# GpSimd adds the mean row of the normalised tiles, and the residual's moves are dealt out 6, 6, 6, 6, 5, 3

## The chip, the cores and the metric

The kernel runs on one core of a Trainium2 chip. The metric is the device time of one execution in microseconds (us); the figure for a kernel is the median of its runs. The engines are TensorE (PE in the profile, with its weight loads as PEld), VectorE (DVE), ScalarE (ACT), GpSimd (POOL) and SyncE (SP), which here only issues transfers. Each engine works through its own instructions in the order in which they were put there; an instruction whose inputs are not ready holds up everything behind it on that engine.

## The reference, cut to what matters

One decoder layer on 256 tokens of width 2048, with 16 meta tokens ahead of them: sparse attention and causal pooling side by side, an output map, a layer norm, a gated feed-forward block with a causal convolution of width 3, and a second layer norm.

```python
mix = jnp.concatenate([attn_out, pool_out], axis=-1) @ w_o[l]
h = layer_norm(ALPHA * h + mix, ln1_g[l], ln1_b[l])
f = conv_gated_ffn(h, w_up[l], conv_w[l], conv_b[l], w_down[l])
h = layer_norm(ALPHA * h + f, ln2_g[l], ln2_b[l])

def layer_norm(x, g, b):
    mu = jnp.mean(xf, axis=-1, keepdims=True)
    var = jnp.mean(jnp.square(xf - mu), axis=-1, keepdims=True)
    return (xf - mu) * lax.rsqrt(var + LN_EPS) * g + b
```

The change lies between the first layer norm and the end of the up-projection's first third.

## The kernel before, in words

Features lie on the 128 partitions and tokens along the free axis: `y` (the profile calls it x) holds 16 tiles `y[:, m]` of 128 features x 272 tokens. Every fp32 weight block `wraw` of 128x2048 comes in by a 1 MB transfer from SP, is rounded by ACT in two halves of 1024 columns (L162) into the high part of `whl`, and DVE subtracts the high part from the raw weight for the low part (L163), also in two halves. There are three `whl` buffers. A product (L202 to L204) then runs 16 steps k of three matmuls each: high x high, high x low, low x high. So the third matmul of a product waits for the first L163 of its block.

The up-projection has 44 steps f with two halves each (`half_` 0 and 1), one weight block and 48 matmuls for each half. The norm of the first layer norm is not ready when the first up-projections start. The first four f (`FOLDED = 4`) therefore multiply weights with the tiles `folded`, which hold the values before the norm times the gain, and `unfold` puts the norm in behind the product: `u = ps * rs` on DVE (L731), a row `w` from ACT (L733), and `u = u + w` on GpSimd (L734). `rs` is the row of reciprocal deviations, `m2` the row of minus mean times that; both are halves of the tile `of_token`, written by ACT at L695. The convolution starts with L721 on ACT, which reads `u`, and goes on with L722 and L723 on DVE; `gate` follows (L738, L739).

Meanwhile `normalise(m)` makes the real inputs `hp` of the later up-projections, three tiles after each half of the first f: a multiplication by `rs` on GpSimd (L703), an addition of `m2` on DVE (L704), gain and offset on ACT (L705), the high part on ACT (L707), the low part on DVE (L708). They are first used by f = 4.

At f = 4 and 5 the 16 tiles of `y` are transposed in blocks of 32x32 on DVE (L869). At f = 6 to 11, `residual` carries the transposed blocks into `y2`, the accumulator of the output with tokens on partitions, in 32 transfers issued on ACT's queue (L715): the list `moves` has the 16 for the first 128 tokens ahead of the 16 for the others. The down-projection of the first eight f runs between the up-projections of the next eight (`seven`); its results are added into `y2` by DVE at L799, which therefore waits for these transfers.

The order on each engine comes from a scheduler that works with its own priorities and estimates, so instructions written in one place may stand elsewhere in the queue. What belongs to a product, and so its weight block, is told below by f and half: f1h1 is the second half of f = 1.

Of the kernel before, what the change touches and what calls it, by code (L numbers as in the profile page):

```python
# [14 lines left out]
ALU = mybir.AluOpType  # L15
# [21 lines left out]
FOLDED = 4  # L37
# [61 lines left out]
def tile_layer(ctx, tc, xt, w_first, w_proj, w_uk, w_uv, w_pool, w_o, w_up, w_down, cols, rows, rel_bias, onehot, out):  # L99
    nc = tc.nc  # L100
# [4 lines left out]
    def act_tile(name, n=T):  # L105
        t = ring.tile([P, SLOT], F32R, tag="act", name=name)
        u, l = NARROW if n < T else (0, T)
        return Pair(t[:, u:u + n], t[:, l:l + n])
# [4 lines left out]
    def big():  # L113
        return pm.tile([P, 512], F32, tag="mm", name="mm")
# [75 lines left out]
    def weights(ahead=2):  # L190
        i = state["use"]
        state["use"] += 1
        prefetch(i + 1 + ahead)
        return ready.pop(i)

    def product(ps, hl, m, act, lo, hi, ks=range(KT), width=P, k0=0, k1=KT):

        for n in range(k0, k1):
            k = ks[n]
            wh, wl = hl[:, 0, k * width:k * width + m], hl[:, 1, k * width:k * width + m]  # L200
            ah, al = act[k][:, 0, lo:hi], act[k][:, 1, lo:hi]
            nc.tensor.matmul(ps, wh, ah, start=n == 0, stop=False)  # L202
            nc.tensor.matmul(ps, wh, al, start=False, stop=False)  # L203
            nc.tensor.matmul(ps, wl, ah, start=False, stop=n == KT - 1)  # L204
# [36 lines left out]
    def col(base, j):  # L241
        return cv[:, base + j:base + j + 1]
# [31 lines left out]
    for i in range(2):  # L274
        nc.vector.tensor_tensor(kidx[DI * i:DI * i + DI, 1 + i, :], ps[:DI, :T], kidx[:DI, 0, :].bitcast(F32),
                                op=ALU.subtract)
# [356 lines left out]
    rs, m2 = of_token[:, :NQ], of_token[:, NQ:]  # L633
# [42 lines left out]
    def deviation():  # L676
        ps = small()
        column_sums([s1], cuts, 0, ps)
        column_sums([s2], cuts, 1, ps)
        for i, (a, b) in enumerate(cuts):  # L680
            r = slice(0, b - a)
            nc.vector.tensor_scalar_mul(st[r, 0, i:i + 1], ps[r, 64 * i:64 * i + 1], 1.0 / D)
            nc.vector.tensor_scalar(st[r, 1, i:i + 1], ps[r, 64 * (3 + i):64 * (3 + i) + 1], 1.0 / D, EPS,
                                    op0=ALU.mult, op1=ALU.add)
        nc.vector.tensor_tensor(st[:, 2, :], st[:, 0, :], st[:, 0, :], op=ALU.mult)
        nc.vector.tensor_tensor(st[:, 1, :2], st[:, 1, :2], st[:, 2, :2], op=ALU.subtract)
        nc.vector.tensor_tensor(st[:2, 1, 2:], st[:2, 1, 2:], st[:2, 2, 2:], op=ALU.subtract)
        nc.gpsimd.tensor_tensor(st[:, 2, :], st[:, 1, :], half, op=ALU.pow)
        nc.vector.scalar_tensor_tensor(st[:, 3, :], st[:, 0, :], -1.0, st[:, 2, :], op0=ALU.mult, op1=ALU.mult)

    def deviation_rows():
        for j, dst in ((2, rs), (3, m2)):
            ps = small()
            spread(st[:, j, :], cuts, ps)
            nc.scalar.activation(dst, ps[:, :NQ], AF.Copy)  # L695
# [5 lines left out]
    def normalise(m):  # L701
        yd = y[:, m, Q0:]
        nc.gpsimd.tensor_tensor(yd, yd, rs, op=ALU.mult)  # L703
        nc.vector.tensor_tensor(yd, yd, m2, op=ALU.add)  # L704
        nc.scalar.activation(yd, yd, AF.Identity, bias=col(LN1, 2 * m + 1), scale=col(LN1, 2 * m))  # L705
        a = act_tile("hp", NQ)
        nc.scalar.activation(a[:, 0, :NQ], yd, AF.Copy)  # L707
        nc.vector.tensor_tensor(a[:, 1, :NQ], yd, a[:, 0, :NQ].bitcast(F32), op=ALU.subtract)  # L708
        h_parts.append(a)
# [9 lines left out]
    def conv(j, half_, src, za):  # L719
        z = fp.tile([P, S], F32, name="z", tag="z1", bufs=1) if half_ else za  # L720
        nc.scalar.activation(z, src[:, 2:NQ], AF.Identity, bias=col(C_B, j), scale=col(C_W, 3 * j + 2))  # L721
        nc.vector.scalar_tensor_tensor(z, src[:, 1:NQ - 1], col(C_W, 3 * j + 1), z, op0=ALU.mult, op1=ALU.add)  # L722
        nc.vector.scalar_tensor_tensor(z, src[:, :S], col(C_W, 3 * j), z, op0=ALU.mult, op1=ALU.add)  # L723
        return z

    def unfold(ps):

        sc = fp.tile([P, 2], F32, name="sc", tag="sc")
        nc.vector.tensor_copy(sc, ps[:, NQ:NE])
        u = fp.tile([P, NQ], F32, name="u", tag="sq")  # L730
        nc.vector.tensor_tensor(u, ps[:, :NQ], rs, op=ALU.mult)  # L731
        w = fp.tile([P, NQ], F32, name="w", tag="acc", bufs=2)
        nc.scalar.activation(w, m2, AF.Identity, bias=sc[:, 1:], scale=sc[:, :1])  # L733
        nc.gpsimd.tensor_tensor(u, u, w, op=ALU.add)  # L734
        return u

    def gate(za, zg):
        nc.scalar.activation(za, za, AF.Gelu_apprx_tanh)  # L738
        nc.vector.tensor_tensor(za, za, zg, op=ALU.mult)  # L739

    def two_parts(a, src):
        nc.scalar.activation(a[:, 0], src, AF.Copy)
        nc.vector.tensor_tensor(a[:, 1], src, a[:, 0].bitcast(F32), op=ALU.subtract)
        return a
# [7 lines left out]
    def forms(p, r, j):  # L752

        a11, a21, a12, a22 = r[:, 0, :P], r[:, 0, P:], r[:, 1, :P], r[:, 1, P:]
        s = fp.tile([P, 4 * P], F32, name="forms", bufs=1).rearrange("p (a b) -> p a b", b=P)
        nc.gpsimd.tensor_tensor(s[:, 0], a21, a22, op=ALU.add)
        nc.gpsimd.tensor_tensor(s[:, 2], s[:, 0], a11, op=ALU.subtract)
        nc.gpsimd.tensor_tensor(s[:, 1], a12, s[:, 2], op=ALU.subtract)
        nc.gpsimd.tensor_tensor(s[:, 3], a11, a21, op=ALU.subtract)  # L759
        left = two_parts(slot(), r[:, :, :P])  # L760
        mid = two_parts(slot(), s[:, :2])
        right = ring.tile([P, SLOT], F32R, tag="act", name="right")
        right = Pair(*(right[:, o:o + 2 * P].rearrange("p (b c) -> p b c", c=P) for o in (0, T)))
        right = two_parts(right, s[:, 2:])
        if p == PLAIN[0]:
            lone, i = two_parts(slot(), r[:, :, P:]), 1
        else:
            if j % 2 == 0:
                held["lone"] = slot()
            lone, i = held["lone"], j % 2  # L770
            two_parts(lone[:, :, i], a22)
        return {"P1": (left, 0), "P2": (left, 1), "P5": (mid, 0), "P3": (mid, 1), "P6": (right, 0),
                "P7": (right, 1), "P4": (lone, i), "a21": (lone, 0)}
# [52 lines left out]
    for item in plan:  # L826
        if item[0] in "ABC":
            seven(*item)
            continue
        _, f, half_ = item  # L830
        part = next(p for p in range(len(PARTS)) if f < sum(PARTS[:p + 1]))
        if half_ == 0:
            if f % 2 == 0:
                pair = fp.tile([P, 2, S], F32, name="za", tag="z0", bufs=3)
            both = []
        hl = weights()
        ps = big()
        if todo and f > FOLDED - 1 + half_:
            p, r = todo.pop(0)
            pairs[p].append(forms(p, r, len(pairs[p])))  # L840
        if f < FOLDED:
            k = 0
            if f + half_ == 0:
                product(ps[:, :NE], hl, P, folded, 0, NE, k1=7)
                deviation()
                product(ps[:, :NE], hl, P, folded, 0, NE, k0=7, k1=14)
                deviation_rows()
                k = 14
            product(ps[:, :NE], hl, P, folded, 0, NE, k0=k)
            while len(h_parts) < min(KT, 3 * (2 * f + half_ + 1)):  # L850
                normalise(len(h_parts))
            both.append(ps)
            if half_ == 0:
                continue
            both = [conv(i * FT + f, i, unfold(both[i]), pair[:, f % 2]) for i in range(2)]
        else:
            product(ps[:, :NQ], hl, P, h_parts, 0, NQ)
            both.append(conv(half_ * FT + f, half_, ps, pair[:, f % 2]))
            if half_ == 0:
                continue  # L860
        gate(*both)
        if part == len(PARTS) - 1:
            a = fp.tile([P, 2, NE], F32R, name="gp", tag="gp", bufs=19)
            gated.append(two_parts(a[:, :, :S], both[0]))
        elif f % 2:
            todo.append((part, pair))
        if f in (FOLDED, FOLDED + 1):
            for m in range(8 * (f - FOLDED), 8 * (f - FOLDED) + 8):
                nc.vector.transpose(y[:, m, NM:], y[:, m, NM:])  # L869
        if FOLDED + 2 <= f < FOLDED + 8:  # L870
            for _ in range((6, 5, 5)[f % 3]):
                residual(*moves.pop(0))


# [176 lines left out]
```

## Time and profile before

| what | us |
|---|---|
| runs, median (lowest to highest of 3) | 1038.26 (1037.95 to 1040.22) |
| the profiled execution's own time | 1039.8 |
| its span, first to last instruction | 1038.0 |
| PE busy in the span | 1025.3 (99%) |
| DVE / ACT / POOL busy | 886.1 (85%) / 617.4 (59%) / 209.3 (20%) |

The profiled execution is 1.5 us above the median and 1.8 us above its own span. Its granted TensorE clock is 0.998 of full over the span. Times in the profile count from the span's first instruction. In rows of the timeline the first column is the start, the second the length (of all the instructions that the row merges, up to the end of the last), x is their count, and the bracket gives the idle time of the engine ahead of it and what ended it. Ends of matmuls are modelled, so stalls of PE are better read from the distance of starts than from its busy share.

### The profile page before, as it was taken

How to read it: one execution, taken by the hardware profiler on the slowest of the kernel's cores; microseconds unless marked ns; L12 is line 12 of the kernel's file. 1: busy time of each engine (PE TensorE's matmuls, PEld its weight loads, DVE VectorE, ACT ScalarE, POOL GpSimd, SP SyncE). 2: the span in 40 equal slices, each digit the busy share in tenths (PEclk: the TensorE clock that was granted, in tenths of full speed). 3: DMA queues.
4: the chain of work that ended last, by engine and by line, in shares of the span. 5: the costliest groups of instructions: out<-in, count | busy, mean ns of one | idle time of the engine just before them, and what ended most of it. 6: DMA issues, size and time to landing. Idle time of an engine off the chain costs nothing.

```text
span 1038.0 us, 19165 instructions
## 1 busy us (share of the span) xinstructions
PE 1025.3 (99%) x7649; PEld 973.8 (94%) x7649; DVE 886.1 (85%) x1372; ACT 617.4 (59%) x994; POOL 209.3 (20%) x262
## 2 busy tenths in 40 slices
PE   9999999999999999999999999999999999999996
PEld 8998999999999999998999999999999999999985
DVE  6879468758779997898999999899998998999866
ACT  7566356645447765565566655656555656566654
POOL 1100014125345311211122011120111201110022
PEclk9999999999999999999999999999999999999999
DMA  9766543454552587898798787887878878898766
GB/s 326 259 216 236 194 156 109 152 188 167 191 196 85 200 233 248 261 301 257 260 299 293 283 283 271 287 284 274 286 269 288 276 277 278 269 306 274 277 203 152
DMA packets 59610, 250.80 MB, mean 242 GB/s; under 512 B 21718, under 2 KB 22400, under 8 KB 32384
## 3 DMA queue, kind: packets, MB, share of 16 engines
q1 hardware_dynamic: 34016, 229.37, 61.5%
q0 software_dynamic: 8320, 17.71, 8.9%
q10 hardware_dynamic: 17184, 2.49, 1.4%
q8 instruction: 60, 0.98, 0.4%
q14 instruction: 30, 0.25, 0.1%
HBM read 233.55 MB, written 3.16 MB: 228 GB/s over the span
## 4 chain that ended last, share of the span: by engine, by line
PE 82%; DVE 7%; issue 5%; DMA 4%; POOL 1%; ACT 1%; DVEq 0%; POOLq 0%; ACTq 0%
PE mm L204 20%; PE mm L203 20%; PE mm L202 20%; PE at L792 5%; PE at L793 5%; PE at L791 5%; DVE whl L163 3%; DMA wraw<-in_w_down 2%; DMA wraw<-in_w_up 1%; DMA y<-x 1%; DVE x L704 1%; ACT whl L162 1%; DVE hp L708 1%; PE mm L265 1%; PE mm L267 1%
## 5 line engine op out<-in xcount | busy, mean ns | idle before, releaser
L163 DVE TENSOR_TENSOR whl<-wraw,whl 128x1024 fp32r<-128x1024 f32 (+1 forms) x418 | 492.7, 1213 | 53.8 <-ACT whl L162 52.9
L162 ACT ACTIVATE whl<-wraw 128x1024 fp32r<-128x1024 f32 (+1 forms) x418 | 405.0, 1014 | 147.4 <-DVE wraw L158 39.6
L204 PE MATMUL mm<-hp,whl 128*128 128x258 f32 x1280 | 360.8, 282 | 0.0
L203 PE MATMUL mm<-hp,whl 128*128 128x258 f32 x1280 | 359.7, 281 | 0.0
L202 PE MATMUL mm<-hp,whl 128*128 128x258 f32 x1280 | 355.5, 278 | 0.0
L202 PEld LDWEIGHTS mm<-hp,whl 128*128 128x128 f32 x1280 | 240.7, 188 | 3.1
L203 PEld LDWEIGHTS mm<-hp,whl 128*128 128x128 f32 x1280 | 239.6, 187 | 3.0
L204 PEld LDWEIGHTS mm<-hp,whl 128*128 128x128 f32 x1280 | 240.2, 188 | 0.0
L202 PE MATMUL mm<-xp,whl 128*128 128x256 f32 (+5 forms) x384 | 110.9, 289 | 0.0
L203 PE MATMUL mm<-xp,whl 128*128 128x256 f32 (+5 forms) x384 | 108.5, 282 | 0.0
L204 PE MATMUL mm<-xp,whl 128*128 128x256 f32 (+5 forms) x384 | 108.1, 282 | 0.0
L791 PE MATMUL at<-whl,gp 128*128 128x512 f32 x212 | 83.8, 395 | 0.9 <-DVE y L799 0.9
L792 PE MATMUL at<-whl,gp 128*128 128x512 f32 x212 | 83.8, 395 | 0.1
L793 PE MATMUL at<-whl,gp 128*128 128x512 f32 x212 | 83.4, 394 | 0.0
L203 PEld LDWEIGHTS mm<-xp,whl 128*128 128x128 f32 x384 | 72.3, 188 | 0.8 <-issue 0.5
L202 PEld LDWEIGHTS mm<-xp,whl 128*128 128x128 f32 x384 | 72.2, 188 | 0.6
L204 PEld LDWEIGHTS mm<-xp,whl 128*128 128x128 f32 x384 | 72.2, 188 | 0.3 <-DVE whl L163 0.2
L759 POOL TENSOR_TENSOR forms<-za 128x128 f32<-128x128 f32 x20 | 20.2, 1011 | 226.6 <-DVE za L739 212.1
L721 ACT ACTIVATE z<-mm,cv 128x256 f32<-128x256 f32 x40 | 22.5, 564 | 71.1 <-PE mm L204 70.2
L791 PEld LDWEIGHTS at<-whl,gp 128*128 128x128 f32 x212 | 39.8, 188 | 9.5 <-DVE y L799 1.4
L793 PEld LDWEIGHTS at<-whl,gp 128*128 128x128 f32 x212 | 39.8, 188 | 9.3
L721 ACT ACTIVATE za<-mm,cv 128x256 f32<-128x256 f32 x40 | 22.4, 560 | 43.6 <-PE mm L204 43.6
(316 smaller groups left out, 1854.6 us busy)
## 6 DMA issues: line engine op xcount, KB each, us to landing
wraw<-in_w_up SPq DMA_DIRECT2D x88, 1024.0 KB, 5.1
wraw<-in_w_down SPq DMA_DIRECT2D x80, 1024.0 KB, 6.8
wraw<-in_w_proj SPq DMA_DIRECT2D x24, 1024.0 KB, 5.1
wraw<-in_w_o SPq DMA_DIRECT2D x16, 1024.0 KB, 4.9
y<-v POOLq DMA_DIRECT2D x27, 256.0 KB, 8.5
y<-u POOLq DMA_DIRECT2D x18, 256.0 KB, 4.8
wraw<-in_w_first SPq DMA_DIRECT2D x8, 304.0 KB, 5.4
x<-in_xt SPq DMA_DIRECT2D x1, 2176.0 KB, 8.4
```

Of the source, the lines that this page charges most:

```text
L162: nc.scalar.activation(hl[:, 0, c], raw[:, c], AF.Copy)
L163: nc.vector.tensor_tensor(hl[:, 1, c], raw[:, c], hl[:, 0, c].bitcast(F32), op=ALU.subtract)
L202: nc.tensor.matmul(ps, wh, ah, start=n == 0, stop=False)
L203: nc.tensor.matmul(ps, wh, al, start=False, stop=False)
L204: nc.tensor.matmul(ps, wl, ah, start=False, stop=n == KT - 1)
L265: nc.tensor.matmul(ps[:m, :T], wh, x_parts[k][:, 0, :], start=k == 0, stop=False)
L267: nc.tensor.matmul(ps[:m, :T], wl, x_parts[k][:, 0, :], start=False, stop=k == KT - 1)
L721: nc.scalar.activation(z, src[:, 2:NQ], AF.Identity, bias=col(C_B, j), scale=col(C_W, 3 * j + 2))
L759: nc.gpsimd.tensor_tensor(s[:, 3], a11, a21, op=ALU.subtract)
L791: nc.tensor.matmul(ps, a[:, 0, i], hl[:, 0, w], start=fresh, stop=False)
L792: nc.tensor.matmul(ps, a[:, 0, i], hl[:, 1, w], start=False, stop=False)
L793: nc.tensor.matmul(ps, a[:, 1, i], hl[:, 0, w], start=False, stop=last)
```

## The change

Two edits. In `normalise` the addition of `m2` goes from DVE to GpSimd, so GpSimd does both the multiplication and the addition of each of the 16 tiles. And the 32 moves of the residual are dealt out over f = 6 to 11 as 6, 6, 6, 6, 5, 3 where they were 6, 5, 5, 6, 5, 5.

```diff
     def normalise(m):
         yd = y[:, m, Q0:]
         nc.gpsimd.tensor_tensor(yd, yd, rs, op=ALU.mult)
-        nc.vector.tensor_tensor(yd, yd, m2, op=ALU.add)
+        nc.gpsimd.tensor_tensor(yd, yd, m2, op=ALU.add)
         nc.scalar.activation(yd, yd, AF.Identity, bias=col(LN1, 2 * m + 1), scale=col(LN1, 2 * m))
...
         if FOLDED + 2 <= f < FOLDED + 8:
-            for _ in range((6, 5, 5)[f % 3]):
+            for _ in range((6, 6, 6, 6, 5, 3)[f - FOLDED - 2]):
                 residual(*moves.pop(0))
```

GpSimd's queue behind the first layer norm's statistics (L688), before: the 16 multiplications, then the first two additions of `unfold`.

```order
L688 TENSOR_TENSOR st<-st,half 128x3
L703 TENSOR_TENSOR x<-x,of_token 128x258 x16
L734 TENSOR_TENSOR u<-u,w 128x258 x2
L759 TENSOR_TENSOR forms<-za 128x128
L734 TENSOR_TENSOR u<-u,w 128x258 x2
```

The end of the same stretch after; ahead of it stand three multiplications, three additions, and then five more blocks of two multiplications and two additions.

```order
L703 TENSOR_TENSOR x<-x,of_token 128x258 x2
L704 TENSOR_TENSOR x<-x,of_token 128x258 x2
L703 TENSOR_TENSOR x<-x,of_token 128x258
L704 TENSOR_TENSOR x<-x,of_token 128x258
L734 TENSOR_TENSOR u<-u,w 128x258 x2
L759 TENSOR_TENSOR forms<-za 128x128
```

All 32 operations of the normalisation now stand ahead of the first L734; before, 16 did.

ACT's queue at the end of the moves (f = 11), before:

```order
L162 ACTIVATE whl<-wraw 128x1024 x2
L738 ACTIVATE za<-za 128x256
L715 DMA y_3789<-x 32x16x32 x2
L721 ACTIVATE z<-mm,cv 128x256
L715 DMA y_3789<-x 32x16x32
L162 ACTIVATE whl<-wraw 128x1024 x4
```

and after:

```order
L162 ACTIVATE whl<-wraw 128x1024 x2
L738 ACTIVATE za<-za 128x256
L715 DMA y_3789<-x 32x16x32
L721 ACTIVATE z<-mm,cv 128x256
L162 ACTIVATE whl<-wraw 128x1024 x4
```

The last move now stands ahead of the last L721 of that step, where before two stood there and one behind it. The first moves go forward too. ACT's queue at the first move, after:

```order
L721 ACTIVATE za<-u,cv 128x256
L738 ACTIVATE za<-za 128x256
L715 DMA y_3789<-x 32x16x32
L733 ACTIVATE w<-of_token,sc 128x258
L162 ACTIVATE whl<-wraw 128x1024
L721 ACTIVATE z<-u,cv 128x256
```

Before, no move stood there: L162 came right behind that L738, and the first two moves 12 instructions behind it; the transposes on DVE that the move waits for are likewise earlier.

## The prediction

> **What bounds the kernel now.** The page's first part comes first: TensorE is busy for the whole span, so only what makes it wait, or ends its waits, can move the time.
>
> ```profile
> PE 1025.3 (99%) x7649; PEld 973.8 (94%) x7649; DVE 886.1 (85%) x1372; ACT 617.4 (59%) x994; POOL 209.3 (20%) x262
> ```
>
> The view of waits, for PE between 300 and 520 us, names what it waits for where the change acts (a third row, of 0.2, lies ahead of it); the timeline gives the starts.
>
> ```profile
> PE mm L204 <- DVE whl L163: 1.0, 2, 0.6
> PE at L791 <- DVE y L799: 0.9, 1, 0.9
> ...
> 328.17 0.28 PE L203 MATMUL mm<-fold,whl 128*128 128x260 f32 x1
> 328.92 0.39 PE L204 MATMUL mm<-fold,whl 128*128 128x260 f32 x1 [0.47 <-DVE whl L163]
> ...
> 340.32 0.28 PE L202 MATMUL mm<-fold,whl 128*128 128x260 f32 x1
> 340.44 0.28 PE L203 MATMUL mm<-fold,whl 128*128 128x260 f32 x1
> 341.29 0.39 PE L204 MATMUL mm<-fold,whl 128*128 128x260 f32 x1 [0.57 <-DVE whl L163]
> ...
> 469.30 0.39 PE L792 MATMUL at<-whl,gp 128*128 128x512 f32 x1
> 469.53 0.40 PE L793 MATMUL at<-whl,gp 128*128 128x512 f32 x1
> 470.85 0.50 PE L791 MATMUL at<-whl,gp 128*128 128x512 f32 x1 [0.92 <-DVE y L799]
> ```
>
> Three stalls, by distances of starts. 328.17 to 328.92 is 0.75 where a step of 260 columns is 0.12 (340.32 to 340.44): 0.63 lost. 340.44 to 341.29: 0.73. 469.53 to 470.85 is 1.32 where a step of 512 is 0.23: 1.09. Together 2.45 us: that is all this change can win. The first two are the third matmuls of the products f2h0 and f3h0, which wait for the low half of their weight block. Neither block has slack, so what delays it delays the kernel. What makes the first block late stands on ACT, DVE and POOL:
>
> ```profile
> 309.54 1.25 POOL L703 TENSOR_TENSOR x<-x,of_token 128x258 f32<-128x258 f32 x2 [1.72 <-ACT of_token L695]
> 309.54 13.87 POOL L703 TENSOR_TENSOR x<-x,of_token 128x258 f32<-128x258 f32 x16 [1.72 <-ACT of_token L695]
> 323.37 1.81 POOL L734 TENSOR_TENSOR u<-u,w 128x258 f32<-128x258 f32 x2
> ...
> 324.33 0.60 ACT L721 ACTIVATE za<-u,cv 128x256 f32<-128x256 f32 x1 [0.72 <-POOL u L734]
> 325.21 0.60 ACT L721 ACTIVATE z<-u,cv 128x256 f32<-128x256 f32 x1 [0.28 <-POOL u L734]
> 325.72 1.99 ACT L162 ACTIVATE whl<-wraw 128x1024 fp32r<-128x1024 f32 x2
> ...
> 326.06 0.47 DVE L722 SCALAR_TENSOR_TENSOR za<-u,cv,za 128x256 f32<-128x256 f32 x1
> 327.25 0.48 DVE L723 SCALAR_TENSOR_TENSOR z<-u,cv,z 128x256 f32<-128x256 f32 x1
> 327.65 2.35 DVE L163 TENSOR_TENSOR whl<-wraw,whl 128x1024 fp32r<-128x1024 f32 x2
> ```
>
> Read upwards: PE waits for L163; it stands behind the convolution on DVE, and its input L162 behind both L721 on ACT; these wait for the two L734; and these stand behind the 16 multiplications on POOL, which run without a gap from 309.54. So POOL's queue already sets that stall. Neither L162 nor L721 changes its place on ACT, so 16 more POOL operations push this block.
>
> **The addition's move: how late POOL gets.** Alone, a 128x258 operation costs POOL 0.60: two take 1.25, one alone is 0.65 long (the minimum below). Beside DVE it costs more:
>
> ```profile
> L703 POOL TENSOR_TENSOR x<-x,of_token x16: 647/826/1624, 309.5 to 322.6; 128x258 f32<-128x258 f32 x16
> ...
> 310.51 3.70 DVE L704 TENSOR_TENSOR x<-x,of_token 128x258 f32<-128x258 f32 x5 [2.49 <-ACT of_token L695]
> 320.46 2.44 DVE L708 TENSOR_TENSOR hp<-x,hp 128x258 fp32r<-128x258 f32 x3
> 332.10 1.09 DVE L704 TENSOR_TENSOR x<-x,of_token 128x258 f32<-128x258 f32 x3
> 333.11 1.22 DVE L163 TENSOR_TENSOR whl<-wraw,whl 128x1024 fp32r<-128x1024 f32 x1
> 337.46 1.08 DVE L869 STREAM_TRANSPOSE x<-x 128x256 f32<-128x256 f32 x3
> ```
>
> The median 0.826, less the overlap of 0.04 that a pair shows (2 x 0.647 against 1.25), is a pitch of 0.79, +0.19 beside a DVE operation of this size; the maximum 1.62 is the two beside an L163, +0.97. As a test: 16 x 0.60, the two L163 and the twelve L704 and L708 in that stretch (the rows at 310.51 and 320.46 are the first and the last of them) give 9.6 + 1.9 + 2.3 = 13.8 us, against 13.87 in the row. After the change no L704 is left on DVE; until POOL is through, DVE has six L708 (tiles 0 to 5, all that ACT can make before its L721) and two L163. The six transposes that move into the stretch I take to cost POOL nothing, since they read one tile and not two; the trace has none beside L703, and at +0.19 each they would add 1.1. So 32 x 0.60 + 6 x 0.19 + 2 x 0.97 = 22.3 us: POOL is through at 331.8 instead of 323.4.
>
> The bounds of this sum: with no disturbance at all 19.2 us, end 328.7; with each operation at 0.79 and the two L163, 26.9 us, end 336.5. I take 331.8, since the price by kind reproduces the row.
>
> From there: two L734 alone, 0.60 + 0.65, put the second L721 at 333.1, 7.9 later than 325.21. L162 follows at 333.6, and lasts 1.0 a half. DVE is idle by then, where before it came to L722 only at 326.06, after L704 work: L722, L723 and L723 (0.40 apart) after L721's end at 333.7, L163 from 334.9 to 336.1. PE goes on at 336.15 instead of 328.92: 7.2 later, after having waited from 328.05.
>
> **The next block.** ACT has no slack behind this.
>
> ```profile
> 325.70:340.60 14.90, 14.43 (x119) 14.13 (x118) 14.90 (x35) 14.47 (x26) 2.04 (x3) 1.00 0.42 141
> ...
> 338.19 0.60 ACT L721 ACTIVATE z<-u,cv 128x256 f32<-128x256 f32 x1 [0.32 <-POOL u L734]
> 340.02 1.22 DVE L163 TENSOR_TENSOR whl<-wraw,whl 128x1024 fp32r<-128x1024 f32 x1
> ```
>
> In the row of the windows the columns are PE, PEld, DVE, ACT and POOL: ACT is busy 14.47 of 14.90 us, so it shifts as a whole by 7.9, and with it L163 of f3h0: PE cannot pass its third matmul there before 341.29 + 7.9 = 349.2. By its own work it would be there at 336.15 + (340.44 + 0.12 - 328.92) = 347.8, if its clock stays full. It may not:
>
> ```profile
> 1.10 2.31 PE L124 MATMUL at<-warm 128*128 128x256 bf16 x10 [1.10 <-POOL warm L121]
> 5.31 0.61 PE L267 MATMUL mm<-xp,whl 128*80 128x272 f32 x2
> 5.76 0.29 PE L266 MATMUL mm<-xp,whl 128*128 128x272 f32 x1
> ...
> 1028.52 0.28 PE L900 MATMUL at<-whl,gp 128*128 128x256 f32 x1
> ...
> 1030.00:1035.00 5.00, 0.00 (x0) 0.00 (x0) 3.03 (x6) 0.00 (x0) 0.56 (x1) 0.82 1.03 257
> 1035.00:1038.00 3.00, 0.00 (x0) 0.00 (x0) 0.00 (x0) 0.00 (x0) 0.00 (x0) 0.50 0.35 126
> ```
>
> The last matmul ends at 1028.8; a mean granted clock of 0.82 between 1030 and 1035 with 0.50 at its end puts the fall 1.8 us before 1035, 4.4 us after it. And at the start PE has half speed from 1.10 to about 5.75 (0.23 a step of 272 before, 0.125 after). A wait of some 7 us is longer than 4.4, so I take the clock to fall and half of 4.65 us, 2.3, to be lost: 347.8 + 2.3 = 350.1. The later of 349.2 and 350.1 counts: 8.8 us behind 341.29. The bounds of the clock's price are 0 (349.2, +7.9) and a whole 4.65 (352.5, +11.2).
>
> The Trainium skill, TensorE: Matmul & The Clock Gate, Part 1, says that an idle window of about 3.4 us halves the clock and a busy one restores it. The trace agrees on the fall; by the page's window the loss would be an estimated 1.7 us and the total 1045.4.
>
> **DVE's relief.** DVE loses 16 L704, 0.34 apart in the row at 332.10. That wins nothing by itself: it waits for ACT, and ACT for POOL. Behind 341 us its blocks come with the same delay as PE, so no new stall.
>
> **The moves.** DVE's L799 is what PE awaits at 470.85:
>
> ```profile
> 456.01 2.73 ACTq L715 DMA_DIRECT2D y<-x  x2
> 460.82 0.59 ACTq L715 DMA_DIRECT2D y<-x  x1
> 463.67 2.62 DVE L163 TENSOR_TENSOR whl<-wraw,whl 128x1024 fp32r<-128x1024 f32 x2
> 469.51 0.69 DVE L799 SCALAR_TENSOR_TENSOR y<-y,v 128x512 f32<-128x512 f32 x1 [3.22 <-issue]
> ...
> DMA to landing us min/median/max: 2.3/4.8/9.7
> ```
>
> DVE is ready at 466.29 and waits 3.22 us. The last move is issued at 460.82; its landing within 8.7 is what fits. After, the last one stands where one was issued at 456.01, so even at the maximum of 9.7 it lands by 465.7 (plus the common delay): L799 at 466.3, its successors done before PE needs their bank. That wins the 1.09. At the other end nothing is won. At the front, a move now holds up L733 and L162 on ACT until DVE's last transposes are through: two at 0.36, and an issue of 0.59, about 1 us. I take this at nothing: the next blocks are wanted only two products later; its other end is +1.0.
>
> **Sum.** +8.8 - 1.1 = +7.7 us on the profiled execution, whose span is 1038.0 and whose time of 1039.8 lies 1.5 above the median; put on the median of 1038.26: 1046.0 us.
>
> **Rivals.** *The clock does not fall*: 349.2 counts, +7.9 - 1.1, 1045.1. For it: the wait is not one pause, since two matmuls run once the high half is there, about 1.3 us before its end.
>
> *POOL at the disturbed pitch throughout*: end 336.5, second L721 at 338.3 (1.8 behind, as before), L163 done at 341.3; PE is at the third matmul of f3h0 at 341.3 + 11.6 + 2.3 = 355.2, +13.9 - 1.1: 1051.1. Against it: DVE has hardly work left there.
>
> *The engines take turns wholly*: every L708 costs POOL 0.34 and every L163 1.14 (its 1.22 less the overlap): 19.2 + 2.0 + 2.3 = 23.5, end 333.0, 1.2 later: 1047.2. The same price for before gives 9.6 + 4.1 + 2.3 = 16.0 against 13.87, which speaks against it. The Trainium skill, SBUF — State Buffer, Who interferes with whom, has this rule, an exclusive lock on a shared port; the trace does not bear it out in full.
>
> *The moves win nothing*: 1047.1; a late landing is possible, since the wait has no named releaser.
>
> *Faster*: the weight block does not hang on POOL, as it would if L734 could start before the 16 additions or L162 stood ahead of L721. Then DVE's relief ends the two stalls and the moves the third: 1038.26 - 2.45 = 1035.8. It is decided at 323.4: POOL would have to be through by then with 32 operations, 0.43 each, against the 0.60 of the undisturbed pair.
>
> **How the numbers follow.** A measurement of this kernel can tell about 0.2%, 2.1 us, from no change. Forecast, 1046.0: 0.48. Clock stays: 0.20. Turns: 0.06. Moves win nothing: 0.08. POOL disturbed throughout: 0.10. Faster: 0.04. Within 0.2% (some of the delay is caught up unseen): 0.04. The range from 1042.5 to 1049.5 leaves out the last three, 0.18; its lower end is POOL undisturbed (3.1 earlier, 1042.9), its upper one the clock's full price (+2.4) and the first move's 1.0 on ACT. Faster 0.04, same 0.04, slower 0.92.
>
> **What would show it.** In the profile after: L703 and L704 on POOL from 309.5 to about 332; L734 there; a gap of PE from 328.05 to about 336 named DVE L163, or ACT L162 for its first part; a granted clock under 1 between 330 and 342; no L799 among PE's waits. The prediction is wrong if L162 of that block starts well before 333, or if POOL's 32 operations take under 19 us.

## The result, and the profile after

The changed kernel takes 1048.95 us (1048.42 to 1050.09, 4 runs) against 1038.22 for the kernel before (1037.95 to 1040.22, 4 runs): a ratio of 1.0102, 95% interval 1.0089 to 1.0114. It is slower by some 10.7 us, forecast were 7.7. The profiled execution took 1048.77 us, its span is 1047.0; by the two profiles the difference is 9.0.

The busy row of the page of the changed kernel:

```profile
PE 1027.4 (98%) x7649; PEld 976.7 (93%) x7649; DVE 879.7 (84%) x1356; ACT 619.0 (59%) x994; POOL 218.7 (21%) x278
```

And PE's rows in its view of waits between 300 and 520 us (us in all, times, longest; a third row is that of 0.2 ahead of the change):

```profile
PE mm L202 <- ACT whl L162: 8.3, 1, 8.3
PE mm L204 <- DVE whl L163: 0.7, 1, 0.7
```

POOL has 9.4 us more work, and DVE 6.4 less. One wait of PE of 8.3 us on ACT is new, and the row with L799 is gone. The same chain as before, in the timeline of the changed kernel, from POOL up to PE:

```profile
309.57 1.85 POOL L703 TENSOR_TENSOR x<-x,of_token 128x258 f32<-128x258 f32 x3 [1.72 <-ACT of_token L695]
...
333.54 1.42 POOL L734 TENSOR_TENSOR u<-u,w 128x258 f32<-128x258 f32 x2
334.99 0.60 ACT L721 ACTIVATE z<-u,cv 128x256 f32<-128x256 f32 x1
335.50 1.99 ACT L162 ACTIVATE whl<-wraw 128x1024 fp32r<-128x1024 f32 x2
336.42 0.48 DVE L723 SCALAR_TENSOR_TENSOR z<-u,cv,z 128x256 f32<-128x256 f32 x1
336.82 2.36 DVE L163 TENSOR_TENSOR whl<-wraw,whl 128x1024 fp32r<-128x1024 f32 x2
...
327.96 0.28 PE L204 MATMUL mm<-fold,whl 128*128 128x260 f32 x1
336.59 0.58 PE L202 MATMUL mm<-fold,whl 128*128 128x260 f32 x1 [8.35 <-ACT whl L162]
338.09 0.59 PE L204 MATMUL mm<-fold,whl 128*128 128x260 f32 x1 [0.70 <-DVE whl L163]
```

POOL starts its 32 operations at 309.57 and reaches the first L734 at 333.54 instead of 323.37. L721, L162 and L163 follow one behind the other, and PE, which ended f1h1 at 328.2, starts f2h0 at 336.59 and does its third matmul at 338.09, where it was at 328.92: 9.2 us later. Meanwhile the clock fell. Windows of 1 us, PE alone (the columns behind the window: its length, PE busy, granted clock, DMA share, GB/s):

```profile
330.00:331.00 1.00, 0.00 (x0) 0.58 0.00 0
...
343.00:344.00 1.00, 1.00 (x8) 0.60 0.32 131
```

All rows between these have 0.50, the ones around them 1.00. A mean of 0.58 puts the fall at 330.16, 1.9 us after the last matmul's end; 0.60 puts the rise at 343.80, 7.2 us after PE is at work again.

A sum over PE's matmuls serves as a ledger below: the distance from each start to the next, less the median distance for that width, added up over a stretch. It holds stalls and clock losses alike. Spans less their whole sums agree to 1.2 us (1025.2 to 1026.4) in all kernels here except the one with added matmuls.

| kernel | median us | 320 to 360 | 360 to 400 | 400 to 480 |
|---|---|---|---|---|
| before | 1038.2 | 1.6 | -0.1 | 1.3 |
| changed | 1048.95 | 12.4 | -0.1 | 0.0 |
| before, once more | 1039.37 (one run) | 1.6 | -0.1 | 0.0 |
| the moves alone | 1043.66 | 1.6 | -0.1 | 4.9 |
| changed, first L734 pair on DVE | 1043.87 | 5.7 | -0.1 | 0.0 |
| changed, PE kept busy | 1053.3 | 8.1 | 1.5 | 0.0 |
| changed, another place in POOL's queue | 1044.9 | 7.1 | -0.1 | 0.0 |
| before, ten additions on POOL behind L734 | 1042.14 | 5.3 | -0.1 | 0.0 |
| changed, the two operations swapped | 1048.29 (one run) | 11.4 | 0.0 | 0.0 |
| both operations on DVE | 1051.96 | 0.9 | 0.1 | 11.6 |
| before, all L734 on DVE | 1047.24 | 0.0 | -0.1 | 8.2 |
| before, L734 of f = 0 on DVE | 1039.0 | 1.4 | 0.1 | 0.0 |
| before, L734 of f = 0 and 1 on DVE | 1042.15 | 0.0 | 1.2 | 2.4 |
| the same, moves 8, 6, 4, 4, 4, 6 | 1039.3 | 0.0 | 1.2 | 2.0 |

### The profile page after: what moved, and what is told of

Its sections match the earlier page's. It is cut to its first block, busy times and chain, and to the rows that moved or that the text cites. A ratio compares the mean times of both kernels' runs of the same rounds, so it can differ in the third digit from the quotient of the medians.

```text
span 1047.0 us, 19162 instructions
## 1 busy us (share of the span) xinstructions
PE 1027.4 (98%) x7649; PEld 976.7 (93%) x7649; DVE 879.7 (84%) x1356; ACT 619.0 (59%) x994; POOL 218.7 (21%) x278
## 4 chain that ended last, share of the span: by engine, by line
PE 91%; POOL 3%; issue 3%; DVE 1%; ACT 1%; POOLq 0%; DVEq 0%; ACTq 0%
PE mm L204 23%; PE mm L203 23%; PE mm L202 22%; PE at L792 6%; PE at L793 6%; PE at L791 5%; POOL x L704 1%; POOL x L703 1%; PE mm L265 1%; PE mm L267 1%; PE mm L266 1%; PE at L362 0%; PE mm L485 0%; PE at L363 0%; POOL gb L883 0%
## 5 line engine op out<-in xcount | busy, mean ns | idle before, releaser
L163 DVE TENSOR_TENSOR whl<-wraw,whl 128x1024 fp32r<-128x1024 f32 (+1 forms) x418 | 493.3, 1214 | 56.2 <-ACT whl L162 55.2
L162 ACT ACTIVATE whl<-wraw 128x1024 fp32r<-128x1024 f32 (+1 forms) x418 | 404.2, 1014 | 122.9 <-DVE wraw L158 33.6
L792 PE MATMUL at<-whl,gp 128*128 128x512 f32 x212 | 83.6, 395 | 0.0
L721 ACT ACTIVATE z<-mm,cv 128x256 f32<-128x256 f32 x40 | 22.6, 564 | 84.9 <-PE mm L204 84.9
L759 POOL TENSOR_TENSOR forms<-za 128x128 f32<-128x128 f32 x20 | 19.7, 985 | 227.3 <-DVE za L739 219.4
L721 ACT ACTIVATE za<-mm,cv 128x256 f32<-128x256 f32 x40 | 22.5, 564 | 51.7 <-PE mm L204 51.6
L793 PEld LDWEIGHTS at<-whl,gp 128*128 128x128 f32 x212 | 39.8, 188 | 9.4
L756 POOL TENSOR_TENSOR forms<-za 128x128 f32<-128x128 f32 x20 | 22.9, 1143 | 120.3 <-DVE za L739 120.3
```

Source lines behind the costliest of these rows:

```text
L162: nc.scalar.activation(hl[:, 0, c], raw[:, c], AF.Copy)
L163: nc.vector.tensor_tensor(hl[:, 1, c], raw[:, c], hl[:, 0, c].bitcast(F32), op=ALU.subtract)
L792: nc.tensor.matmul(ps, a[:, 0, i], hl[:, 1, w], start=False, stop=False)
L793: nc.tensor.matmul(ps, a[:, 1, i], hl[:, 0, w], start=False, stop=last)
```

## The experiments

The kernel before, run beside the first group of these, took 1038.42 us; beside the later ones 1038.56, 1038.48 and 1038.7.

### Is the stall at L799 always there?

The kernel before, without an edit.

> The kernel before, profiled a second time. Theory (the moves' stall is chance): the first profile's 1039.8 us lies 1.6 above most runs (1037.95 to 1038.26) because its stalls behind 460 us, 1.09 at 470.85 and 0.35 at 513.1, are not in a usual run; then this profile shows 1038.2 us or so with PE's steps regular there, and the changed kernel loses its only gain when it is set against the median: 9.0 us between the two profiles, 10.7 between the medians. Rival: the stall at L799 is in each execution and the 1.6 us lie elsewhere; then the row PE <- DVE y L799 is here again at about 0.9.

It took 1039.37 us. PE's waits between 280 and 530 us (a second row, 0.2 for L248, lies outside the stretch):

```profile
PE mm L204 <- DVE whl L163: 1.0, 2, 0.6
```

The two early stalls are there to a hundredth; the one on L799 isn't. It is there in one execution of this program and absent in another, so its absence in the changed kernel can't be put down to the change. This execution's span is only 0.4 us shorter for it, since PE lost 1.1 us more in its first 60 us than in the profiled one.

The queues say more on the moves: with the addition on POOL and the moves dealt out as before, every queue reads as in the changed kernel, instruction for instruction. (The experiment on the place in POOL's queue, below, has that dealing; in its trace ACT, DVE, PE and SP keep the order of the changed kernel.) The second edit changes nothing once the first is made. That the moves stand earlier in the changed kernel is the scheduler's answer to the first.

### The moves alone

```diff
-            for _ in range((6, 5, 5)[f % 3]):
+            for _ in range((6, 6, 6, 6, 5, 3)[f - FOLDED - 2]):
```

> The moves dealt out 6, 6, 6, 6, 5, 3, the addition on DVE as before. Theory (the whole delay comes from POOL's queue): no delay, 1036.5 to 1038.3 us: the two early stalls of 0.63 and 0.73 stay, the stall at L799 goes where an execution has it. Rival (the moves on ACT's queue hold up weights): slower than before by 1 us or more, with PE waiting for L162 or L163 behind 370 us.

1043.66 us (1041.48 to 1045.26, 5 runs), ratio 1.0047 (1.0033 to 1.0060): slower by 5 us, in the rival's range, where the stretch of the normalisation is untouched. PE's new wait:

```profile
PE at L792 <- DVE whl L163: 3.1, 1, 3.1
```

And the chain of waits that leads to it, between 420 and 470 us (start, length, what):

```profile
427.70 7.06 DMA wraw<-in_w_down
434.78 0.69 DVE wraw L157
...
436.53 0.70 DVE whl L163
437.24 8.08 DMA wraw<-in_w_up
...
446.52 2.37 DVE whl L163 x2
448.91 6.24 DMA wraw<-in_w_down
...
457.05 0.50 PE at L792
```

L157 is the first step on DVE for a down-projection block that has just landed. In this kernel DVE's queue has it ahead of all four L163s of the two blocks before it, so these wait for a transfer that they don't need. The buffer of the older block comes free later, and the next transfer is issued at 437.24. At 455.2 the same happens again, with the block that lands there: L157 starts when its transfer is through, and only then L163, for which PE waits. In the kernel before, run once more, the first of these L157 stands behind two of the four, those that free this buffer; rows of DVE and of SP's queue in its timeline:

```profile
435.14 0.95 DVE L157 TENSOR_TENSOR wraw<-wraw 128x512 f32<-128x512 f32 x1
...
435.25 0.33 SPq L149 DMA_DIRECT2D wraw<-in_w_up  x1
```

and that transfer goes out at 435.25, 2.0 us earlier. The later issue comes from the scheduler's order on DVE. Traffic may have added to it: from issue to landing this transfer took 8.1 us here and 6.8 in the kernel before, one execution each, and this run can't tell whether the moves did that. The last three experiments test the order.

### The first pair of L734 on DVE

```diff
-    def unfold(ps):
+    def unfold(ps, adder=nc.gpsimd):
...
-        nc.gpsimd.tensor_tensor(u, u, w, op=ALU.add)
+        adder.tensor_tensor(u, u, w, op=ALU.add)
...
-            both = [conv(i * FT + f, i, unfold(both[i]), pair[:, f % 2]) for i in range(2)]
+            both = [conv(i * FT + f, i, unfold(both[i], nc.vector if f == 0 else nc.gpsimd), pair[:, f % 2]) for i in range(2)]
```

in the changed kernel, so that f2h0 no longer hangs on POOL.

> The changed kernel, but the two additions of unfold (L734) for f = 0 go to DVE, which is idle there; POOL still does all 32 operations of the normalisation. Theory (the weight block waits because L734 stands behind the 32 operations): L734 runs at about 322.5 on DVE, L162 of f2h0 by 325, no PE wait and no clock fall; both early stalls gone: 1035 to 1037.5 us, faster than before. Rival (the cost is the engines' disturbance, or ACT waiting for the tiles themselves): POOL is as long at work and DVE as disturbed, so 1045 us or more.

1043.87 us (1042.24 to 1045.28, 5 runs), ratio 1.0050 (1.0038 to 1.0063), between the two ranges. The stall ahead of f2h0 is gone and half of the loss with it; 5.4 us stay. PE's wait:

```profile
PE mm L204 <- DVE whl L163: 3.6, 2, 2.0
```

The rows of DVE ahead of the first of the two:

```profile
332.51 1.76 DVE L708 TENSOR_TENSOR hp<-x,hp 128x258 fp32r<-128x258 f32 x2
334.89 1.67 DVE L163 TENSOR_TENSOR whl<-wraw,whl 128x1024 fp32r<-128x1024 f32 x1
```

And two windows of 1 us, PE alone, columns as above:

```profile
336.00:337.00 1.00, 0.39 (x3) 0.94 0.00 0
340.00:341.00 1.00, 1.00 (x10) 0.85 0.99 188
```

Two things are new. DVE is slow: two L708 take 1.76 and an L163 1.67, beside POOL's operations, where an undisturbed L163 is 1.22. And a pause of 2.3 us (starts 334.29 and 336.61) was enough for the clock: by the means it falls at 336.88, after PE has gone on, and rises at 340.30. The second pause, of 1.84, left it alone.

### PE kept busy through the wait

```diff
+            if (f, half_) == (2, 0):
+                busy = small()
+                for _ in range(64):
+                    nc.tensor.matmul(busy[:, :256], warm[:, :P], warm, start=True, stop=True)
```

in the changed kernel, ahead of f2h0.

> The changed kernel, with 64 matmuls of 256 bf16 columns on the warm-up tile (6.9 us at full clock) put on PE between f1h1 and f2h0, into the wait of 8.6 us. Theory (the clock falls because PE is idle, and the next block's weights limit what its return is worth): the granted clock stays 1.00 from 328 to 345, f2h0 takes 5.8 us behind its third matmul at about 338.1 instead of 8.2; of these 2.7 us only about 1.3 are won, since L163 of f3h0 ends at 351.0 and PE then waits for it: 1047.7 us. Rivals: all 2.7 are won (1046.2); or nothing, because the half clock has another cause.

1053.3 us (1053.1 to 1053.9, 4 runs), ratio 1.0142 (1.0128 to 1.0156). As a measurement of the clock's price this failed: with the 64 matmuls the scheduler ordered ACT otherwise, and f3h0 and f3h1 got stalls of their own; behind the second of these the clock fell after all, at 360.74. The windows still show the mechanism (columns: length, PE, PEld, DVE, ACT, POOL, clock, DMA share, GB/s); two of this kernel, and then the last one in the changed kernel:

```profile
328.00:334.00 6.00, 6.00 (x57) 5.37 (x57) 0.00 (x0) 0.00 (x0) 5.92 (x10) 1.00 0.00 0
340.00:346.00 6.00, 6.00 (x52) 6.00 (x52) 5.16 (x12) 6.00 (x13) 0.42 (x1) 1.00 0.53 178
```
```profile
340.00:346.00 6.00, 6.00 (x37) 6.00 (x37) 5.16 (x13) 6.00 (x13) 0.21 (x1) 0.68 0.56 179
```

With PE at work the clock stays at 1.00, and 52 matmuls run between 340 and 346 where 37 did. The fall comes from PE's pause.

### Only the place in POOL's queue

```diff
-        nc.gpsimd.tensor_tensor(yd, yd, rs, op=ALU.mult)
-        nc.vector.tensor_tensor(yd, yd, m2, op=ALU.add)
+        with tc.issue_after(unfolded[3 if m >= 12 else 1]) if m >= 6 else ExitStack():
+            for by, op in (rs, ALU.mult), (m2, ALU.add): nc.gpsimd.tensor_tensor(yd, yd, by, op=op)
```

in the kernel before; `unfolded` lists the L734 as they are made.

> All 16 additions stay on GpSimd as in the changed kernel, and every other engine's queue is word for word that of the changed kernel; only GpSimd's own order differs: the tiles 0 to 5 (12 operations) stand ahead of the first pair of L734, the tiles 6 to 11 between the first and the second pair, the tiles 12 to 15 behind the second. Theory: the loss is the place of L734 behind 32 operations in GpSimd's queue and the clock that falls in the stall; so the 8.5 us stall ahead of f2h0 is gone, L734 starts at about 323.4 as before, the granted clock stays at 1.00 from 320 to 360, and the time is 1037.2 to 1039.2. Rival: additions on GpSimd cost as such, since the later tiles come late (12 operations of about 0.8 are 9.6, so tile 11 is ready at about 334.8, where ACT asks for it at 335.3) and DVE's L708, waiting for them, holds up L163 as in the kernel with the unfolding on DVE: stalls of 2 to 4 us ahead of f2h1 and f3h0, 1040.5 to 1043.

1044.9 us (1043.63 to 1046.3, 5 runs), ratio 1.0056 (1.0037 to 1.0074), above both ranges. Half of each theory: the 8.5 us ahead of f2h0 are gone, with all 32 operations still on POOL and no other queue changed, so L734's place behind them was the cause of that stall. But a new one stands at f3h0's third matmul. PE's wait (a second row has 0.8 for L162, at the start of f3h0):

```profile
PE mm L204 <- DVE whl L163: 3.9, 2, 3.7
```

Rows of POOL and DVE in the timeline:

```profile
323.23 12.12 POOL L704 TENSOR_TENSOR x<-x,of_token 128x258 f32<-128x258 f32 x12
...
341.39 0.96 DVE L722 SCALAR_TENSOR_TENSOR z<-u,cv,z 128x256 f32<-128x256 f32 x1
343.93 1.66 DVE L163 TENSOR_TENSOR whl<-wraw,whl 128x1024 fp32r<-128x1024 f32 x1
```

POOL needs 1.01 for each operation, where one alone is 0.60 to 0.69 (two experiments on); DVE's L722 takes 0.96 instead of 0.47, and L163 1.66 instead of 1.22. The rival had the late tiles as its reason, but DVE's timeline has no idle time from 320 to 347, so they did not hold it up; what the rows show is that POOL and DVE slow each other.

### Ten additions where POOL is idle

```diff
-        nc.vector.tensor_tensor(yd, yd, m2, op=ALU.add)
+        with tc.issue_after(unfolded[1]) if m >= 6 else ExitStack(): (nc.gpsimd if m >= 6 else nc.vector).tensor_tensor(yd, yd, m2, op=ALU.add)
```

> The kernel before with the additions of tiles 6 to 15 alone on GpSimd, queued there behind the first pair of L734; the 16 multiplications ahead of it as before, the first six additions on DVE. Theory (DVE is the engine that ends PE's two small stalls of 0.63 and 0.73 us at 328 and 340, and GpSimd is idle from 325 to 336): ten additions of 0.42 leave DVE, the two stalls shrink, nothing is delayed: 1036.9 to 1038.4, against 1038.4 before. Rival: the additions run beside L163 on DVE and lengthen it (1.66 instead of 1.22 for 1024 columns where GpSimd works beside it), and take back what the additions gave: 1038.4 to 1039.6.

1042.14 us (1041.52 to 1043.65, 10 runs), ratio 1.0030 (1.0020 to 1.0041): worse than either range. L734 starts at 323.82, with no addition ahead of it, and PE waits for L163 three times. Its row in the view of waits, and rows of POOL and DVE in the timeline:

```profile
PE mm L204 <- DVE whl L163: 4.1, 3, 1.7
...
325.41 10.13 POOL L704 TENSOR_TENSOR x<-x,of_token 128x258 f32<-128x258 f32 x10
...
328.15 0.96 DVE L723 SCALAR_TENSOR_TENSOR z<-u,cv,z 128x256 f32<-128x256 f32 x1
329.03 3.43 DVE L163 TENSOR_TENSOR whl<-wraw,whl 128x1024 fp32r<-128x1024 f32 x2
333.28 0.41 DVE L731 TENSOR_TENSOR u<-mm,of_token 128x258 f32<-128x258 f32 x1
333.62 0.43 DVE L869 STREAM_TRANSPOSE x<-x 128x256 f32<-128x256 f32 x1
```

Against the rows of before, L723 goes from 0.48 to 0.96 and the two L163 from 2.35 to 3.43. L731, which reads one operand from PSUM, and L869, which reads one tile, keep their 0.41 and 0.43 although POOL works beside them. An addition that leaves DVE saves it about 0.34 of pitch and costs it 0.5 for each small operation with two tiles in SBUF that runs beside it on POOL. That is the rival's mechanism, at a higher price. The Trainium skill, SBUF — State Buffer, Who interferes with whom, says that a DVE instruction with two SBUF inputs contends with a GpSimd one that reads SBUF, and one with at most one, outside its two-port modes, doesn't; these rows agree.

### The two operations swapped

```diff
-        nc.gpsimd.tensor_tensor(yd, yd, rs, op=ALU.mult)
-        nc.gpsimd.tensor_tensor(yd, yd, m2, op=ALU.add)
+        nc.gpsimd.tensor_tensor(yd, yd, rs, op=ALU.add)
+        nc.gpsimd.tensor_tensor(yd, yd, m2, op=ALU.mult)
```

> The changed kernel with the two operations of normalise swapped on GpSimd (first the addition at L703, then the multiplication at L704), so it computes (x + m2-row) in another order and its numbers differ; all queues are the same. Theory: it is the second operation on a tile that has a pitch of 0.70 where the first has 0.60, whatever it computes: undisturbed L703 0.60 and L704 0.70 again, the end of the 32 operations at 333.5. Rival: an addition costs 0.70 and a multiplication 0.60 on GpSimd: L703 0.70 and L704 0.60, with the same end. By both 1048.4 to 1050.1.

1048.29 us in one run; the kernel computes something else, so only its times count. Two blocks on POOL with DVE idle, of this kernel and then of the changed one:

```profile
330.19 1.24 POOL L703 TENSOR_TENSOR x<-x,of_token 128x258 f32<-128x258 f32 x2
331.39 1.41 POOL L704 TENSOR_TENSOR x<-x,of_token 128x258 f32<-128x258 f32 x2
```
```profile
329.58 1.23 POOL L703 TENSOR_TENSOR x<-x,of_token 128x258 f32<-128x258 f32 x2
330.78 1.40 POOL L704 TENSOR_TENSOR x<-x,of_token 128x258 f32<-128x258 f32 x2
```

From start to start L703 takes 1.20 for two and L704 (to 332.15 in the changed kernel) 1.37, whatever they compute: 0.60 and 0.69. It isn't the addition. Whether it is that L704 reads what L703 has just written, or that its second operand is `m2` and not `rs`, stays open.

### Both operations on DVE

```diff
-        nc.gpsimd.tensor_tensor(yd, yd, rs, op=ALU.mult)
+        nc.vector.tensor_tensor(yd, yd, rs, op=ALU.mult)
```

> The opposite of the change: the 16 multiplications of normalise go to DVE too, so GpSimd has none of its 32 operations. Theory (DVE and GpSimd slow each other wherever both read SBUF, so work moved between them is paid on either): DVE takes on 16 x 0.42 = 6.7 us, and wins back what GpSimd beside it costs it now, L704 0.61 instead of 0.42, L708 0.64 instead of 0.38 and L163 up to 1.66 instead of 1.22, over 16 operations each some 8 us; L722, L723, L708 and L163 are at 0.47, 0.38 and 1.22 throughout, and the time is 1037 to 1040, against 1038.5 before. Rival: the work simply adds up on DVE, which is busy without a gap from 315 to 346: 6.7 us more on it, of which 3 to 6.7 come through to PE: 1041.5 to 1045. The scheduler also orders later instructions otherwise, which may add stalls behind 360 us that belong to neither.

1051.96 us (1050.55 to 1054.14, 4 runs), ratio 1.0133 (1.0115 to 1.0151), far outside both ranges. In the stage in question the theory holds: the ledger has 0.9 where before has 1.6, although DVE has 16 operations more. Groups of instructions on DVE, of this kernel between 305 and 350 us and of before between 310 and 350 (busy in all, mean ns of one, idle before):

```profile
L708 DVE TENSOR_TENSOR hp<-x,hp 128x258 fp32r<-128x258 f32 x14 | 6.0, 457 | 0.1
```
```profile
L708 DVE TENSOR_TENSOR hp<-x,hp 128x258 fp32r<-128x258 f32 x16 | 9.8, 640 | 0.0
```

L708 falls from 640 to 457 ns with POOL's multiplications out of the way. The loss is elsewhere: 11.6 us between 400 and 480, in four stalls on L163 at L792. DVE's queue there has an L154 or L157 ahead of four older L163s in three places; why PE stalls at 412, ahead of them, stays open.

### All L734 on DVE

```diff
-        nc.gpsimd.tensor_tensor(u, u, w, op=ALU.add)
+        nc.vector.tensor_tensor(u, u, w, op=ALU.add)
```

> The kernel before with the eight additions of unfold (L734) on DVE; normalise as before. Theory (the chain from the product to L163 runs by way of GpSimd, 0.92 and 0.90 for the pair; on DVE the pair is 0.84 and needs no change of engine): the two stalls of 0.63 and 0.73 us at 328 and 340 shrink by up to 1 us together: 1037.3 to 1038.6. Rival: eight more operations on the engine that is full there, 3.4 us, hold up L163 elsewhere, or the scheduler's new order does, as with the moves alone: 1039.5 to 1043.

1047.24 us (1044.46 to 1051.67, 6 runs), ratio 1.0084 (1.0064 to 1.0103), beyond both ranges. Both early stalls are gone (0.0 in the ledger), and 8.2 us of new ones lie between 400 and 480. PE's waits:

```profile
PE at L792 <- DVE whl L163: 5.6, 3, 2.5
```

Three stalls, and again three places in DVE's queue with an L154 or L157 ahead of four older L163s: the rival's second reason, at a higher price.

### Three kernels for the order on DVE

The L734 of f = 0 alone on DVE (no such place in the queue):

```diff
-        nc.gpsimd.tensor_tensor(u, u, w, op=ALU.add)
+        (nc.vector if f == 0 else nc.gpsimd).tensor_tensor(u, u, w, op=ALU.add)
```

> The kernel before with only the first pair of L734 (f = 0) on DVE. The rows of DVE behind 400 us stand as before: no L157 ahead of the L163s of the block before it. Theory (the later stalls of the last two kernels come from that order on DVE, not from the unfolding): the stall of 0.63 us at 328 goes, nothing behind 400 us is added: 1037.4 to 1038.2, 0.3 to 0.7 under before. Rival (any move of work between DVE and GpSimd costs several us later on): 1040 or more.

Those of f = 0 and 1, `f < 2` in that line (one such place):

> The kernel before with the first two pairs of L734 on DVE and nothing else; in DVE's queue one L157 now stands ahead of four L163s of the block before it, where in the kernel with all the unfolding on DVE three did, and in the kernel before none. Theory (each such place is one stall of 1.5 to 3.5 us at the first L792 of a block between 410 and 465 us, with part of a half-clock window): the two stalls at 328 and 340 are gone (-1.3), one such stall is added: 1039 to 1042. Rival: the stalls do not follow DVE's order, so none (1036.8 to 1037.8) or three as before (1044 and more).

And these with other moves (none):

```diff
-            for _ in range((6, 5, 5)[f % 3]):
+            for _ in range((8, 6, 4, 4, 4, 6)[f - FOLDED - 2]):
```

> The first two pairs of L734 on DVE and the moves dealt out 8, 6, 4, 4, 4, 6, a deal with which no L157 stands ahead of older L163s in DVE's queue. Theory: both stalls at 328 and 340 are gone and none is added between 400 and 470 us: 1036.6 to 1037.8, some 1.2 under before. Rival: moves of another rhythm cost by their traffic or late landing, whatever the order on DVE: stalls at L799 or at L163 between 400 and 515 us, 1039 to 1044.

The first took 1039.0 us (1038.5 to 1044.82, 11 runs; ratio 1.0009, 0.9999 to 1.0019), the second 1042.15 (1040.73 to 1050.24, 12 runs; 1.0037, 1.0021 to 1.0053), the third 1039.3 (1038.28 to 1046.51, 11 runs; 1.0019, 1.0004 to 1.0034). The times miss their ranges, by 0.8, 0.15 and 1.5 us on the slow side. But the stalls at L792 are none, one and none, as the order said. The one, on DVE of the second kernel:

```profile
453.41 0.69 DVE L157 TENSOR_TENSOR wraw<-wraw 128x512 f32<-128x512 f32 x1 [3.53 <-DMA wraw<-in_w_down]
454.02 2.96 DVE L163 TENSOR_TENSOR whl<-wraw,whl 128x1024 fp32r<-128x1024 f32 x3
```

L157 waits 3.53 us for its transfer, with three L163 behind it that could have run. In the first kernel an L154 at 420.9 waits 2.98 us ahead of only two older ones, and PE does not stall. The hoped-for gain of 1.2 us in the third kernel did not come. Two products behind 360 us have new stalls of 0.3 and 0.7 (the second kernel has them too), and PE waits for L799:

```profile
PE at L791 <- DVE y L799: 1.8, 1, 1.8
```

DVE's row for it in the timeline:

```profile
470.82 0.69 DVE L799 SCALAR_TENSOR_TENSOR y<-y,v 128x512 f32<-128x512 f32 x1 [3.32 <-issue]
```

Its last two moves are issued from 461.27 on, as late as the last one of the kernel before (460.82), and L799 waits as it did there. In the first kernel the stall at f2h0 goes but that at f3h0 grows from 0.73 to 0.92. None of the versions beats the kernel before.

## Why the prediction was right, and where it was off

The direction, the place, the chain (POOL's queue, L734, L721, L162, L163, PE) and the fall of the clock came out as written; the time is inside the range, 2.95 us above the forecast. Two steps make up the miss: the third matmul of f3h0 came 2.2 us later than forecast, and the 1.1 of the moves were for the most part not won. By its steps:

- **POOL through at 331.8**: it was 333.54. The term of 32 x 0.60 was mis-sized: 0.60 holds for the first operation on a tile, and the second has 0.69. For 16 that is 1.4 of the 1.7 us missed. What DVE beside it cost was nearly right: 23.97 less 16 x 0.60 and 16 x 0.69 leaves 3.3, forecast were 3.1.
- **From L734 to PE**: 4.35 us were forecast from POOL's end to the third matmul, 4.55 were measured, since the pair of L734 has the longer pitch too. So 338.09 for 336.15.
- **The clock**: it was to fall 4.4 us after the last matmul, and fell after 1.9; it was to come back after 4.65 us of work, and came back 7.2 after PE's restart. Both had been read from one fall and one rise of one execution, and neither is a fixed delay (the last section has what the falls follow). From the third matmul of f2h0 to that of f3h0 13.95 us were forecast and 14.17 measured. That is close in part by luck: 5.7 us of this stretch, not 4.65, ran at half clock, which costs 2.85 instead of 2.3, and the work itself took 11.3 instead of 11.6.
- **Which limit counts at f3h0**: PE's own work, as forecast (350.1 against 349.2 by ACT and DVE). The row of L163 for that block and PE's third matmul, in the changed kernel:

```profile
349.76 1.22 DVE L163 TENSOR_TENSOR whl<-wraw,whl 128x1024 fp32r<-128x1024 f32 x1
...
352.26 0.29 PE L204 MATMUL mm<-fold,whl 128*128 128x260 f32 x1
```

L163 is through at 350.98, and PE comes at 352.26 without a wait: +10.97 against +8.8 forecast.

- **The moves, -1.1**: this step failed. The stall that it removes is absent in another execution of the kernel before, and the second edit is void beside the first. In the two profiles it is there (9.0 is 10.8 in the stretch from 320 to 360, less 1.3 between 400 and 480 and 0.4 behind it); 10.7 between the medians would fit if most runs of before don't have it, which two profiles can't show. The prediction had put 0.08 on the rival without it.
- **DVE's relief wins nothing**: right in the changed kernel, but for a second reason that the prediction didn't have. Where DVE has work beside POOL, as in the two experiments with the additions behind L734, it loses by the move what it saves and more. The stall hid this.
- **No new stall behind 341**: right.

The rivals with the engines in turns (end 333.0) and with POOL disturbed throughout (336.5) bracket POOL's end, but neither by its mechanism: POOL's last 14 operations, from 324.4 on, had no work of DVE beside them, and turns with the second operation at 0.69 would have ended at an estimated 334.5 (309.57 + 9.6 + 11.04 + 2.0 + 2.3).

## What to carry to other kernels

Work moved to a less busy engine is paid at the end of that engine's queue: ask who stands there, and write their order if they feed the critical chain. GpSimd and VectorE both slow down when both read pairs of tiles from SBUF, so small operations moved between them win little even where GpSimd is idle. And where a scheduler sets the queues, compare them far behind the edit: one operation that waits for a transfer, put ahead of four that don't, cost 2.4 to 3.9 us a place in four kernels here (the ledger's 400 to 480 over the places; the highest holds the stall at 412 too), where 2.45 was all that this change could win.

## What had not been expected of the hardware

- The half-clock time comes in pieces of one length: 3.42 us in the kernel with the first L734 pair on DVE (336.88 to 340.30), 10.24 in the one with the operations swapped (331.80 to 342.04) and 13.64, four times 3.41, in the changed kernel (330.16 to 343.80). The pieces lie on a grid: from the end of the piece to the next fall, behind the last matmul, at 1036.62 in the first of these kernels and 1040.12 in the last, it is 204 times 3.413 us in both. The Trainium skill, TensorE: Matmul & The Clock Gate, Part 1, has windows of 3.4 us that run on their own; these lengths agree.
- What decides, by these traces, is PE's idle time within one such window, not the length of the pause. Counted to the modelled ends, 1.91 us in the window up to 330.15 brought the fall in the changed kernel, and 2.04 in the one up to 336.89 with the first pair on DVE. In the 14 executions here, behind their first 20 us, each window at full clock with 1.91 or more ended in a fall, and none with 1.82 or less did. A pause of 3.27 us in the kernel with both operations on DVE lay across two windows, 1.54 in one and 1.72 in the next, and the clock stayed; PE's rows and their window (length, PE busy, clock, DMA share, GB/s):

```profile
442.15 0.40 PE L791 MATMUL at<-whl,gp 128*128 128x512 f32 x1
445.81 0.50 PE L792 MATMUL at<-whl,right 128*128 128x512 f32 x1 [3.27 <-DVE whl L163]
...
442.00:446.00 4.00, 0.73 (x4) 1.00 0.78 133
```

A window idle for little more than half is enough, and a fall comes only at a window's end. So it can come 1.9 us after the last matmul, as in the changed kernel, or 4.4, as at the end of the kernel before. The clock came back behind windows with 0.18 us of idle time or less; in the changed kernel one with 0.70 (336.98 to 340.39) kept it at half.
- GpSimd's second operation on a tile had a pitch of 0.69 us, the first 0.60, with addition and multiplication in either place.
- Beside GpSimd's additions, DVE operations of some 256 columns with two SBUF inputs went from 0.48 to 0.96 us; those with one stayed at 0.41 and 0.43.
